# A gated layer's tiles 3 to 20: four of seven products summed in one PSUM bank, weight splits on VectorE, engine order written out

## The chip, the cores and the metric

The kernel runs on one core of one Trainium2 chip. The metric is device time in microseconds (us), here of one core. Engines in the profile: PE is TensorE's matmuls and PEld its weight loads, DVE is VectorE, ACT ScalarE, POOL GpSimd, SP the queue that issues DMAs. A difference of about 0.2% can be told from none.

## The reference

One decoder layer on x of 1024 positions by 1024 channels, all in float32: a mixer (forgetting attention, dilated attention, convolution module, output projection), and then the gated layer, which is what changes here, with 2 x 2816 = 2 x 22 x 128 columns in `w_up`:

```python
h2 = rmsnorm(x, ln2_g[l])
u = jnp.einsum('bsd,df->bsf', h2, w_up[l])
u = causal_dwconv(u, ffn_conv_w[l], ffn_conv_b[l])      # 3 taps
hidden = jax.nn.silu(u[..., :D_FF]) * u[..., D_FF:]
x = x + jnp.einsum('bsf,fd->bsd', hidden, w_down[l])
return rmsnorm(x, g_final)
```

## The kernel before

Channels lie on the 128 partitions, positions along the free dimension, in two halves of 512. Every product is made of float32 operands split in two parts, a rounded high part and the low remainder; three matmuls (high x high, high weight x low input, low weight x high input) give one product of a 128x128 weight block (`mm3`, lines 116 to 118).

The gated layer works on 22 tiles of 128 hidden channels, each with a gate half and a value half. `up` (line 891) makes tile j by Winograd's form of Strassen's product: instead of eight block products it takes seven, of weight combinations (`wsum`, line 743) with input combinations that stay in SBUF (`PROD`, line 816). Product 1 takes the input blocks `b11`, 2 `b21`, 3 `b22`, 4 to 7 `t4`, `t1`, `t2`, `t3`. Each product is 4 blocks x 3 matmuls = 12 matmuls of 512 columns into one bank of its own, so a tile is 84 matmuls. Tiles 0 to 2 have their products 1 and 2 made ahead (`early`) and issue 60.

For a tile, SP loads four raw weight blocks `a11`, `a21`, `a22`, `a12` (256 KB each) into a ring of seven slots; VectorE forms `s1`, `s2`, `a11 - a21`, `s4` from them (lines 760 to 766); for each product `wsplit` (line 821) has ScalarE cast the weights to the high part `wh` (line 827) and GpSimd subtract to get the low part `wl` (line 828). There are four buffers for `wh` and `wl`, so a split can start when the product four before it has ended. VectorE combines the seven banks into the tile's two halves `urg` (gate) and `urv` (value) with seven adds and one copy on ScalarE (lines 900 to 907). `gate` (line 930) is the convolution: on each of `urg` and `urv` one ScalarE activation (first tap and bias, line 937) and two VectorE taps (line 939), then Silu on ScalarE (line 941) and a product on VectorE (line 942). The result is kept in DRAM as blocks and combinations of two tiles, formed every second tile (lines 950 to 957), for the down projection that follows.

The order on each engine is chosen by a scheduler from program order and priority; weight loading and splitting run at high priority. Engines take their instructions in order.

```python
        for n in PORD if pre else order:
            w = wsplit(j, n, ws[n])
            M[n] = bank(f"m{n}_{j}")
            prod(M[n], n, w)
            evict()
```

Of the kernel before, what the change touches and what calls it, by code (L numbers as in the profile page):

```python
# [44 lines left out]
# pairs of hidden tiles taken together in w_down; the last NL tiles are multiplied directly  # L45
# [5 lines left out]
# columns of the packed parameter table  # L51
# [9 lines left out]
def hybrid_trunk(ctx: ExitStack, tc: tile.TileContext, xT, par, win, wvf, wo, wup, wdn,  # L61
# [87 lines left out]
    # ==== mixer =========================================================  # L149
    with ExitStack() as cb_:  # L150
# [32 lines left out]
        # x * ln1_g in two parts, and the sum of squares of x  # L183
        order = (12, 14, 13, 15)          # gv0 gg0 gv1 gg1
# [558 lines left out]
    def wsum(j, src=None, n=4):  # L743
        """the weight blocks and their combinations"""
# [58 lines left out]
    g1 = [half_pair(f"g1_{k}", "aacc"[k]) for k in range(4)]      # B12 and B22 before r2  # L803
# [17 lines left out]
    def wsplit(j, n, t, nk=4):  # L821
        with tc.high_priority():
# [26 lines left out]
    g2 = [half_pair(f"g2_{k}", "a") for k in range(4)]            # T3 and T2  # L849
# [29 lines left out]
    def slot_tile(name, shape, dt=F32):  # L879
        """a tile in any slot that is free by now"""  # L880
# [10 lines left out]
    def up(j, pre=None, order=UORD, then=lambda n: None):  # L891
        """gate and value of one tile of the hidden layer"""
# [259 lines left out]
```

## Time and profile before

| | |
|---|---|
| time, median of 3 runs (lowest, highest) | 1353.99 us (1352.52, 1354.97) |
| profiled execution: span from first to last instruction | 1351.2 us |
| what lies around the span (median less span) | 2.8 us |
| PE busy | 1251.2 us (93%), 5809 matmuls |
| PEld, DVE, ACT, POOL busy | 989.3 (73%), 1081.9 (80%), 603.4 (45%), 775.5 us (57%) |
| POOL, low parts `wl` of the up projection (line 828) | 150.3 us and 103.7 us in two groups, 84 and 66 instructions |

Busy time is an average over stages with different limits, so the stretch of tiles 3 to 20 has to be read by itself. Matmuls overlap: one lasts 0.39 us and the next begins 0.23 us after it, so the distance between starts is what a matmul costs.

### The profile page before, as it was taken

The page shows a single profiled execution, that of the slowest core. Times are in us where ns is not written, and L with a number is a line of the kernel's source. Part 1 is how long each engine was busy: PE and PEld are TensorE (multiplying, and loading weights), DVE is VectorE, ACT ScalarE, POOL GpSimd, SP SyncE. Part 2 cuts the span into 40 slices and gives each one's busy share as a digit, 9 for nine tenths or more (in the row PEclk, how much of TensorE's full clock was granted, in tenths as well). Part 3 has the DMA queues.
Part 4 walks back from the last instruction along what each step waited for, and adds up shares of the span by engine and source line. Part 5 has one row for each costly group of instructions (what it writes and reads, how often), then busy time and mean ns, then how long its engine had stood idle before and what let it go on. Part 6 is the DMA issues. An engine that isn't in the chain of part 4 may idle for free.

```text
span 1351.2 us, 17266 instructions
## 1 busy us (share of the span) xinstructions
PE 1251.2 (93%) x5809; PEld 989.3 (73%) x5809; DVE 1081.9 (80%) x1553; ACT 603.4 (45%) x1092; POOL 775.5 (57%) x607
## 2 busy tenths in 40 slices
PE   7898999999999999997798999999999979999996
PEld 5886677777777767774576877777777857787795
DVE  7899796756665676699988888888888889878876
ACT  6423456655555555434433443333423444534333
POOL 4656545554554532457555566656656577767754
PEclk9999899999999999999899999999999989999998
DMA  6002011110010203320132123231222365525213
GB/s 234 17 26 69 16 48 32 32 32 32 16 32 13 66 12 102 106 67 0 39 110 102 60 105 109 95 109 68 96 102 94 103 194 161 188 84 169 61 32 125
DMA packets 56409, 106.70 MB, mean 79 GB/s; under 512 B 5457, under 2 KB 25601, under 8 KB 56321
## 3 DMA queue, kind: packets, MB, share of 16 engines
q1 hardware_dynamic: 55744, 105.32, 23.8%
q8 instruction: 46, 0.75, 0.2%
q14 instruction: 43, 0.34, 0.1%
q10 hardware_dynamic: 576, 0.28, 0.1%
HBM read 82.75 MB, written 22.83 MB: 78 GB/s over the span
## 4 chain that ended last, share of the span: by engine, by line
PE 49%; DVE 17%; issue 16%; POOL 12%; DMA 3%; ACT 2%; POOLq 0%; DVEq 0%; SPq 0%; ACTq 0%
POOL wl L828 8%; PE m L118 4%; PE s L380 4%; PE m L116 3%; PE m L117 3%; PE pt L405 3%; PE d L118 3%; PE s L379 3%; PE d L117 3%; PE d L116 2%; DVE yc L508 2%; PE av L422 2%; PE av L421 2%; POOL VS L280 1%; DMA tr<-td 1%
## 5 line engine op out<-in xcount | busy, mean ns | idle before, releaser
L828 POOL TENSOR_TENSOR wl<-a,wh 128x512 fp32r<-128x512 f32 x84 | 150.3, 1811 | 29.0 <-ACT wh L827 29.0
L828 POOL TENSOR_TENSOR wl<-s,wh 128x512 fp32r<-128x512 f32 x66 | 103.7, 1574 | 99.8 <-ACT wh L827 99.8
L393 POOL TENSOR_SCALAR w<-w,rd 128x128 f32<-128x128 f32 (+3 forms) x96 | 77.4, 811 | 137.7 <-DVE rd L392 81.0
L117 PE MATMUL m<-t,wh 128*128 128x512 f32 x352 | 139.4, 396 | 7.5 <-DVE t L741 7.5
L116 PE MATMUL m<-t,wh 128*128 128x512 f32 x352 | 138.9, 395 | 5.0 <-ACT t L740 4.2
L118 PE MATMUL m<-t,wl 128*128 128x512 f32 x352 | 138.8, 394 | 2.5 <-POOL wl L828 2.5
L118 PE MATMUL m<-b,wl 128*128 128x512 f32 x240 | 97.5, 406 | 23.2 <-POOL wl L828 22.7
L118 PE MATMUL d<-hc,wld 128*128 128x512 f32 x252 | 102.5, 407 | 10.3 <-POOL wld L828 10.2
L410 DVE TENSOR_TENSOR pl<-pt,ph 128x512 fp32r<-128x512 f32 (+1 forms) x120 | 75.0, 635 | 38.5 <-ACT ph L409 35.3
L117 PE MATMUL d<-hc,whd 128*128 128x512 f32 x252 | 101.2, 402 | 3.6 <-DVE hc L979 3.6
L116 PE MATMUL d<-hc,whd 128*128 128x512 f32 x252 | 101.2, 402 | 2.0 <-ACT whd L827 2.0
L390 ACT ACTIVATE w<-w,mn 128x128 f32<-128x128 f32 (+3 forms) x96 | 74.4, 775 | 62.1 <-DVE mn L385 59.0
L939 DVE SCALAR_TENSOR_TENSOR cv<-urv,prm,cv 128x1023 f32<-128x1023 f32 (+1 forms) x44 | 97.7, 2221 | 0.0
L116 PE MATMUL m<-b,wh 128*128 128x512 f32 x240 | 95.5, 398 | 0.2 <-ACT wh L827 0.2
L117 PE MATMUL m<-b,wh 128*128 128x512 f32 x240 | 95.3, 397 | 0.0
L508 DVE SCALAR_TENSOR_TENSOR yc<-gv,prm,yc 128x1023 f32<-128x1023 f32 (+29 forms) x60 | 89.0, 1484 | 0.9
L827 ACT CAST wh<-s 128x512 fp32r<-128x512 f32 x66 | 39.8, 611 | 103.4 <-DVE s L762 86.9
L939 DVE SCALAR_TENSOR_TENSOR cg<-urg,prm,cg 128x1023 f32<-128x1023 f32 (+1 forms) x44 | 65.8, 1495 | 24.5 <-ACT cg L937 24.5
L117 PEld LDWEIGHTS m<-t,wh 128*128 128x128 f32 x352 | 67.0, 190 | 24.0 <-DVE t L741 10.1
L409 ACT CAST ph<-pt 128x512 fp32r<-128x512 f32 (+1 forms) x120 | 63.9, 542 | 44.4 <-PE pt L405 31.6
L116 PEld LDWEIGHTS m<-t,wh 128*128 128x128 f32 x352 | 67.0, 190 | 20.7 <-ACT t L740 4.9
L118 PEld LDWEIGHTS m<-t,wl 128*128 128x128 f32 x352 | 67.1, 191 | 17.4 <-POOL wl L828 3.8
(437 smaller groups left out, 3706.6 us busy)
## 6 DMA issues: line engine op xcount, KB each, us to landing
a<-in_wup SPq DMA_DIRECT2D x88, 256.0 KB, 2.6
tr<-td SPq DMA_DIRECT2D x27, 512.0 KB, 3.8
a_d<-in_wdn SPq DMA_DIRECT2D x48, 192.0 KB, 2.4
td<-cv SPq DMA_DIRECT2D x9, 512.0 KB, 2.6
td<-ta SPq DMA_DIRECT2D x9, 512.0 KB, 2.6
td<-tb SPq DMA_DIRECT2D x9, 512.0 KB, 2.6
x<-in_xT SPq DMA_DIRECT2D x8, 512.0 KB, 3.7
outT<-fo SPq DMA_DIRECT2D x8, 512.0 KB, 2.8
```

Of the source, the lines that this page charges most:

```text
L116: T.matmul(ps, lhsT=wh, rhs=xh[:, sl], start=first, stop=False)
L117: T.matmul(ps, lhsT=wh, rhs=xl[:, sl], start=False, stop=False)
L118: T.matmul(ps, lhsT=wl, rhs=xh[:, sl], start=False, stop=last)
L379: T.matmul(ps[:, 0:m], lhsT=Q[h][:, qsl], rhs=K[h][:, ks], start=True, stop=False)
L380: T.matmul(ps[:, 0:m], lhsT=Q[h][ro, qsl], rhs=KL[ro, ks], start=False, stop=not diag)
L390: A.activation(w[:, 0:nk], w[:, 0:nk], AF.Exp, scale=-1.0, bias=mn, accum_out=den)
L393: G.tensor_scalar(w[:, 0:nk], w[:, 0:nk], rd, 1.0, op0=ALU.mult, op1=ALU.mult)
L409: A.copy(ph[:, 0:w], pt[:, 0:w])
L410: V.tensor_sub(pl[:, 0:w], pt[:, 0:w], ph[:, 0:w].bitcast(F32))
L508: V.scalar_tensor_tensor(y[:, d:], u[:, 0:S - d], col(wc + 30 - d), y[:, d:], op0=ALU.mult, op1=ALU.add)
L828: G.tensor_sub(lo, t, hi.bitcast(F32))
L939: V.scalar_tensor_tensor(cc[:, d:], ur[:, 0:S - d], col(wc + 2 - d), cc[:, d:], op0=ALU.mult, op1=ALU.add)
```

## The change

Tiles 3 to 20 leave `up` for a new function `pipeline`, which writes out, product by product ("slot" by slot), what VectorE, ScalarE and GpSimd do. Tiles 0 to 2 and 21 stay with `up`.

- Products go in the order 1, 4, 6, 7, 5, 2, 3. Products 1, 6, 5 and 3 accumulate in one bank `mA`; only the first clears it. After each of them ScalarE copies the running sum: M1 (`u1`), M1+M6 (first half of `urv`), M1+M6+M5 (second half), M1+M6+M5+M3 (second half of `urg`). VectorE adds the other three banks: four adds in place of seven.
- The weights of a product are split three products ahead (`prep(g + FRONT)`). The low part is made by VectorE for products 6, 7, 5, 2 and 3, by GpSimd for 1 and 4.
- Weight sums, the convolution of the tile before and the stores are put into fixed slots, and the relative order on the three engines is kept by the scheduler (`manual_schedule`), which still merges other work into it. The value half is convolved before the gate half.

Core of the diff (the new `conv_first`, `conv_tap` and `store` hold the old lines of `gate`, cut apart):

```diff
-    def wsplit(j, n, t, nk=4):
+    def wsplit(j, n, t, nk=4, eng=G):
...
-            G.tensor_sub(lo, t, hi.bitcast(F32))
+            eng.tensor_sub(lo, t, hi.bitcast(F32))
...
-    def prod(ps, n, w, x=None):
+    def prod(ps, n, w, x=None, first=True, **kw):
...
-            mm3(ps, w[k], x[k], FULL, k == 0, k == len(w) - 1)
+            mm3(ps, w[k], x[k], FULL, first and k == 0, k == len(w) - 1, **kw)
...
+    SORD = (1, 4, 6, 7, 5, 2, 3)
+    FIRST, FRONT = 3, 3
+    NP = len(SORD)
+
+    def pipeline(n_last):
...
+        def prep(g):
+            j, n = FIRST + g // NP, SORD[g % NP]
+            if j < n_last:
+                hl[g] = wsplit(j, n, raw[j, SRC[n]], eng=G if (g - FRONT) % NP in (4, 5) else V)
...
+        def evict(j, k):
+
+            if k == 0:
+                M[j, "u1"] = cp.tile([P, HALF], F32, tag="rb2", name=f"u1_{j}", bufs=1)
+                A.copy(M[j, "u1"], M[j, "A"])
+            elif k == 2:
+                ur[j] = [None, ur_tile(f"urv{j}")]
+                A.copy(ur[j][1][:, HS[0]], M[j, "A"])
+            elif k == 3:
+                h0 = ur[j][1][:, HS[0]]
+                V.tensor_add(h0, M[j, 7], h0)
+                V.tensor_sub(h0, h0, M[j, 4])
+            elif k == 4:
+                h1 = ur[j][1][:, HS[1]]
+                A.copy(h1, M[j, "A"])
+                V.tensor_add(h1, M[j, 7], h1)
+            elif k == 5:
+                ur[j][0] = ur_tile(f"urg{j}")
+                V.tensor_add(ur[j][0][:, HS[0]], M[j, 2], M[j, "u1"])
+            elif k == 6:
+                A.copy(ur[j][0][:, HS[1]], M[j, "A"])
...
+        for j in range(FIRST, n_last):
+            nxt = j + 1 < n_last
+            for k, n in enumerate(SORD):
...
+                if n in (4, 7, 2):
+                    prod(M[j, n], n, hl[g])
+                else:
+                    prod(M[j, "A"], n, hl[g], first=n == 1, skip_group_check=True)
+                if k:
+                    evict(j, k - 1)
+                elif j > FIRST:
+                    evict(j - 1, 6)
...
+                prep(g + FRONT)
+                if j > FIRST and k < 4:
+                    after(j - 1, k + 1)
+                if j > FIRST and k >= 4 and tail.get(j - 1):
+                    tail[j - 1].pop(0)()
+                if k == 6:
+                    after(j, 0)
+                    if nxt:
+                        wsums(j + 1, 4)
...
-    for j in range(1, NFF - 1):
-        if j in pre:
-            pre[j]["ws"] = wsum(j)
-        up(j, pre.get(j))
+    for j in range(1, FIRST):
+        pre[j]["ws"] = wsum(j)
+        up(j, pre[j])
+    with tc.manual_schedule(engines={nc.vector.engine, nc.scalar.engine, nc.gpsimd.engine}):
+        pipeline(NFF - 1)
     ur_last = up(NFF - 1, then=release)
```

How the order moves, in rows of line, operation, out<-in and shape; a name's first number is the tile, its next the product, the last a buffer number. VectorE in tile 12 before, from the first weight sum of tile 13 to the last:

```order
L760 TENSOR_TENSOR s1_13_8194<-a21_13_8190,a22_13_8192 128x512
L939 SCALAR_TENSOR_TENSOR cv11_8014<-urv11_7884,prm_67,cv11_8014 128x1023
L763 TENSOR_TENSOR a21_13_8190<-a11_13_8188,a21_13_8190 128x512
L939 SCALAR_TENSOR_TENSOR cv11_8014<-urv11_7884,prm_67,cv11_8014 128x1022
L902 TENSOR_TENSOR sc12_8050<-m6_12_8073,sc12_8050 128x512
L942 TENSOR_TENSOR cv11_8014<-cv11_8014,cg11_8013 128x1024
L762 TENSOR_TENSOR s2_13_8196<-s1_13_8194,a11_13_8188 128x512
L952 TENSOR_TENSOR ta5_8023<-cv11_8014,cv10_7859 128x512
L953 TENSOR_TENSOR tb5_8024<-cv10_7859 128x512
L954 TENSOR_TENSOR ta5_8023<-ta5_8023,cv10_7859 128x512
L766 TENSOR_TENSOR s4_13_8201<-a12_13_8199,s2_13_8196 128x512
```

The same engine now, from product 7 of tile 12 (the fourth slot) to its last slot:

```order
L1008 TENSOR_TENSOR s1_13_8096<-a21_13_8034,a22_13_8036 128x512
L828 TENSOR_TENSOR wl12_3_8099<-s4_12_8016,wh12_3_8098 128x512
L1072 TENSOR_TENSOR cv11_8013<-cv11_8013,cg11_8012 128x1024
L1040 TENSOR_TENSOR urv12_8094<-m7_12_8081,urv12_8094 128x512
L1041 TENSOR_TENSOR urv12_8094<-urv12_8094,m4_12_8044 128x512
L1011 TENSOR_TENSOR s2_13_8118<-s1_13_8096,a11_13_8032 128x512
L961 TENSOR_TENSOR ta5_8126<-cv11_8013,cv10_7861 128x512
L962 TENSOR_TENSOR tb5_8127<-cv10_7861 128x512
L1045 TENSOR_TENSOR urv12_8094<-m7_12_8081,urv12_8094 128x512
L1013 TENSOR_TENSOR a21_13_8034<-a11_13_8032,a21_13_8034 128x512
L966 TENSOR_TENSOR ta5_8126<-ta5_8126,cv10_7861 128x512
L1048 TENSOR_TENSOR urg12_8166<-m2_12_8130,u1_12_8057 128x512
```

Before, s2 of tile 13 stood behind two taps and a product of tile 11; now the splits `wl` have come in, the adds of a tile's banks have become fewer, and the weight sums stand one to a slot. ScalarE now, in tile 12 from the cast for its product 2 on:

```order
L827 CAST wh12_2_8076<-a12_12_7987 128x512
L1037 COPY urv12_8094<-mA_12_8018 128x512
L827 CAST wh12_3_8098<-s4_12_8016 128x512
L1071 ACTIVATE cg11_8012<-cg11_8012 128x1024
L827 CAST wh13_1_8120<-a11_13_8032 128x512
L1044 COPY urv12_8094<-mA_12_8018 128x512
L827 CAST wh13_4_8148<-a22_13_8036 128x512
```

The copies of `mA` stand between casts, and one of them behind the Silu (line 1071) of the tile before; before, ScalarE copied only M1 (line 900). VectorE where tile 2 hands over to tile 3, now:

```order
L903 TENSOR_TENSOR urv2_6483<-m5_2_6544,sc2_6484 128x512
L1016 TENSOR_TENSOR s4_3_6603<-a12_3_6601,s2_3_6598 128x512
L828 TENSOR_TENSOR wl3_6_6614<-s2_3_6598,wh3_6_6613 128x512
L828 TENSOR_TENSOR wl3_7_6637<-a21_3_6592,wh3_7_6636 128x512
L904 TENSOR_TENSOR urg2_6482<-m3_2_6508,urv2_6483 128x512
L906 TENSOR_TENSOR urv2_6483<-m5_2_6544,urv2_6483 128x512
L907 TENSOR_TENSOR urv2_6483<-urv2_6483,m4_2_6564 128x512
L936 SCALAR_TENSOR_TENSOR cg2_6578<-urg2_6482,prm_67,cg2_6578 128x1023
L828 TENSOR_TENSOR wl3_5_6656<-s1_3_6596,wh3_5_6655 128x512
```

Two splits of tile 3 have moved ahead of three adds of tile 2, and a third in among its taps. Elsewhere the order is the same but for a few neighbours: at the very start ScalarE squares the first tile of x ahead of its two casts (lines 209 and 201), with both halves of its load issued first.

## Rows read from the trace of the kernel before

**Rows 1.** Busy time by stretch: us, each engine's busy us (instructions), granted clock, DMA.

```profile
core 0: us, PE busy (x) PEld busy (x) DVE busy (x) ACT busy (x) POOL busy (x), PEclk, DMA share, GB/s
...
690.74:1070.14 379.40, 353.44 (x1513) 285.77 (x1512) 324.47 (x322) 140.26 (x200) 228.43 (x137) 0.99 0.28 96
...
801.53:820.57 19.04, 19.04 (x86) 15.77 (x84) 16.63 (x17) 7.09 (x11) 9.38 (x6) 1.00 0.19 69
...
1089.34:1150.00 60.66, 51.06 (x188) 38.75 (x188) 55.91 (x68) 30.75 (x55) 44.72 (x32) 0.89 0.57 182
```

**Rows 2.** Timeline of PE (start us, us): around first matmuls of tiles 3, 8, 21.

```profile
690.51 0.39 PE L118 MATMUL m<-t,wl 128*128 128x512 f32 x1
690.74 0.39 PE L116 MATMUL m<-b,wh 128*128 128x512 f32 x1
...
801.53 0.39 PE L116 MATMUL m<-b,wh 128*128 128x512 f32 x1
801.75 0.39 PE L117 MATMUL m<-b,wh 128*128 128x512 f32 x1
...
1070.14 0.39 PE L116 MATMUL m<-b,wh 128*128 128x512 f32 x1
```

**Rows 3.** Costliest groups, whole span: xcount | busy us, mean ns | idle before.

```profile
L118 PE MATMUL m<-t,wl 128*128 128x512 f32 x352 | 138.8, 394 | 2.5 <-POOL wl L828 2.5
L118 PE MATMUL m<-b,wl 128*128 128x512 f32 x240 | 97.5, 406 | 23.2 <-POOL wl L828 22.7
```

**Rows 4.** Waits in 690.7 to 1070.1 us: total us, times, longest.

```profile
POOL wl L828 <- ACT wh L827: 106.3, 65, 5.0
ACT wh L827 <- DVE s L762: 86.9, 15, 6.2
...
PE m L118 <- POOL wl L828: 24.5, 12, 2.8
```

**Rows 5.** Durations of DVE lines: minimum/median/maximum ns, first to last start us.

```profile
L939 DVE SCALAR_TENSOR_TENSOR cv<-urv,prm,cv x44: 1269/2311/2333, 667.3 to 1136.7; 128x1023 f32<-128x1023 f32 x22, 128x1022 f32<-128x1022 f32 x22
L763 DVE TENSOR_TENSOR a<-a,a x22: 675/1774/1782, 569.1 to 1061.2; 128x512 f32<-128x512 f32 x22
L942 DVE TENSOR_TENSOR cv<-cv,cg x22: 1207/1708/2306, 676.1 to 1138.0; 128x1024 f32<-128x1024 f32 x22
L902 DVE TENSOR_TENSOR sc<-m,sc x22: 674/678/680, 659.0 to 1088.7; 128x512 f32<-128x512 f32 x22
```

**Rows 6.** Timeline of DVE, and of POOL, in 775 to 805 us.

```profile
776.27 0.68 DVE L952 TENSOR_TENSOR ta<-cv,cv 128x512 f32<-128x512 f32 x1
776.87 0.68 DVE L953 TENSOR_TENSOR tb<-cv 128x512 f32<-128x512 f32 x1
...
791.59 1.77 DVE L763 TENSOR_TENSOR a<-a,a 128x512 f32<-128x512 f32 x1
...
789.06 7.70 POOL L828 TENSOR_TENSOR wl<-a,wh 128x512 fp32r<-128x512 f32 x4 [0.35 <-ACT wh L827]
```

**Rows 7.** Groups of ACT in 690.74 to 1070.14 us, columns as in rows 3.

```profile
L827 ACT CAST wh<-a 128x512 fp32r<-128x512 f32 x72 | 42.8, 615 | 24.5 <-issue 11.9 <-POOL wl L828 6.3 <-PE m L117 6.3
...
L937 ACT ACTIVATE cg<-urg,prm 128x1024 f32<-128x1024 f32 x18 | 22.4, 1244 | 57.9 <-DVE urg L901 50.1 <-DVE urg L904 7.8
...
L941 ACT ACTIVATE cg<-cg 128x1024 f32<-128x1024 f32 x19 | 20.2, 1062 | 58.9 <-DVE cg L939 58.9
L900 ACT COPY sc<-m 128x512 f32<-128x512 f32 x18 | 10.4, 576 | 0.0
```

**Rows 8.** Group of POOL in the same stretch.

```profile
L828 POOL TENSOR_TENSOR wl<-a,wh 128x512 fp32r<-128x512 f32 x73 | 130.3, 1809 | 13.3 <-ACT wh L827 13.3
```

**Rows 9.** DMA issues: KB each, median us from issue to landing.

```profile
a<-in_wup SPq DMA_DIRECT2D x88, 256.0 KB, 2.6
```

**Rows 10.** Timeline of PE at the kernel's start.

```profile
5.04 0.76 PE L116 MATMUL gv0a<-xh,wh_w 128*128 128x512 f32 x1 [5.04 <-DVE wh_w L100]
...
9.31 0.80 PE L116 MATMUL gg0a<-xh,wh_w 128*128 128x512 f32 x1 [1.22 <-DVE wh_w L100]
```

More of the change, by code (lines that the diff above doesn't have):

```diff
@@ L111, in load_chunk, with mm3 @@
         return w
-    def mm3(ps, w, x, sl, first, last):
+    def mm3(ps, w, x, sl, first, last, **kw):
         wh, wl = w
         xh, xl = x
-        T.matmul(ps, lhsT=wh, rhs=xh[:, sl], start=first, stop=False)
-        T.matmul(ps, lhsT=wh, rhs=xl[:, sl], start=False, stop=False)
-        T.matmul(ps, lhsT=wl, rhs=xh[:, sl], start=False, stop=last)
+        T.matmul(ps, lhsT=wh, rhs=xh[:, sl], start=first, stop=False, **kw)
+        T.matmul(ps, lhsT=wh, rhs=xl[:, sl], start=False, stop=False, **kw)
+        T.matmul(ps, lhsT=wl, rhs=xh[:, sl], start=False, stop=last, **kw)
     def mm_gen(ps, ws, xs, sl):
@@ L928, in hybrid_trunk, with conv_first @@
     cvs = {}
[L930 to L937 removed]
+    def conv_first(j, ur, cc, v):
+        wc = C_FW + 3 * (NFF * v + j)
+        A.activation(cc, ur, AF.Identity, scale=col(wc + 2), bias=col(C_FB + NFF * v + j))
@@ new lines, in conv_tap, with cg_tile, cv_tile, store @@
+    def conv_tap(j, ur, cc, v, d):
+        wc = C_FW + 3 * (NFF * v + j)
+        V.scalar_tensor_tensor(cc[:, d:], ur[:, 0:S - d], col(wc + 2 - d), cc[:, d:],
+                               op0=ALU.mult, op1=ALU.add)
+    def cg_tile(j):
+        return cp.tile([P, S], F32, tag="rb", name=f"cg{j}", bufs=1)
+    def cv_tile(j):
+        cvs[j] = x_tile(f"cv{j}")
+        return cvs[j].rearrange("p i s -> p (i s)")
+    def store(j):
+        if j >= LAST:
+            return [lambda: nc.sync.dma_start(hd[j - LAST], cvs[j].rearrange("p i s -> p (i s)"))]
+        if j % 2 == 0:
+            return []
+        p, b1, b2 = j // 2, cvs.pop(j - 1), cvs.pop(j)
+        b11, b12, b21, b22 = b1[:, 0], b1[:, 1], b2[:, 0], b2[:, 1]
+        tiles = []
+        def diffs():
+            nc.sync.dma_start(td[p][:, 0, :], b11)
+            nc.sync.dma_start(td[p][:, 5:7, :], b2)
+            tiles.extend((x_tile(f"ta{p}"), x_tile(f"tb{p}")))
+            ta, tb = tiles
+            V.tensor_sub(ta[:, 1], b22, b12)
+            V.tensor_sub(tb[:, 0], b12, b11)
+        def sums():
+            ta, tb = tiles
+            V.tensor_add(ta[:, 0], ta[:, 1], b11)
+            nc.sync.dma_start(td[p][:, 1:3, :], ta)
+        def rest():
+            ta, tb = tiles
+            G.tensor_sub(tb[:, 1], ta[:, 0], b21)
+            nc.sync.dma_start(td[p][:, 3:5, :], tb)
+        return [diffs, sums, rest]
@@ new lines, in hybrid_trunk, with load, wsums, tile_of @@
+    SORD = (1, 4, 6, 7, 5, 2, 3)
+    FIRST, FRONT = 3, 3
+    NP = len(SORD)
+    def pipeline(n_last):
+        wts, hl, M, ur, raw = {}, {}, {}, {}, {}
+        tail = {}
+        def load(j, b):
+            src = {11: wup[j][:, 0:4], 12: wup[j][:, 4:8], 21: wup[NFF + j][:, 0:4], 22: wup[NFF + j][:, 4:8]}[b]
+            raw[j, b] = raw_tile(f"a{b}_{j}")
+            nc.sync.dma_start(raw[j, b], src)
+        def wsums(j, n):
+            a11, a12, a21, a22 = (raw.get((j, b)) for b in (11, 12, 21, 22))
+            if n == 1:
+                raw[j, "s1"] = raw_tile(f"s1_{j}")
+                V.tensor_add(raw[j, "s1"], a21, a22)
+            elif n == 2:
+                raw[j, "s2"] = raw_tile(f"s2_{j}")
+                V.tensor_sub(raw[j, "s2"], raw[j, "s1"], a11)
+            elif n == 3:
+                V.tensor_sub(a21, a11, a21)
+            else:
+                raw[j, "s4"] = raw_tile(f"s4_{j}")
+                V.tensor_sub(raw[j, "s4"], a12, raw[j, "s2"])
+        SRC = {1: 11, 4: 22, 6: "s2", 7: 21, 5: "s1", 2: 12, 3: "s4"}
+        def prep(g):
+            j, n = FIRST + g // NP, SORD[g % NP]
+            if j < n_last:
+                hl[g] = wsplit(j, n, raw[j, SRC[n]], eng=G if (g - FRONT) % NP in (4, 5) else V)
+        def tile_of(j):
+            if j not in ur:
+                ur[j] = [None, None]
+            return ur[j]
+        def evict(j, k):
[18 more added lines that the diff above has]
+                A.copy(ur[j][0][:, HS[1]], M[j, "A"])
+        gated = {}
+        def after(j, n):
+            urg, urv = ur[j]
+            if n == 0:
+                gated[j] = (cg_tile(j), cv_tile(j))
+            cg, cv = gated[j]
+            if n == 0:
+                conv_first(j, urv, cv, 1)
+                conv_tap(j, urv, cv, 1, 1)
+            elif n == 1:
+                conv_first(j, urg, cg, 0)
+                conv_tap(j, urv, cv, 1, 2)
+            elif n == 2:
+                conv_tap(j, urg, cg, 0, 1)
+            elif n == 3:
+                conv_tap(j, urg, cg, 0, 2)
+            elif n == 4:
+                A.activation(cg, cg, AF.Silu)
+                V.tensor_mul(cv, cv, cg)
+                tail[j] = store(j)
+        for b in (11, 21, 22):
+            load(FIRST, b)
+        for n in (1, 2, 3):
+            wsums(FIRST, n)
+        load(FIRST, 12)
+        wsums(FIRST, 4)
+        for g in range(FRONT):
+            prep(g)
+        for j in range(FIRST, n_last):
+            nxt = j + 1 < n_last
+            for k, n in enumerate(SORD):
+                g = (j - FIRST) * NP + k
+                if k == 0:
+                    M[j, "A"] = bank(f"mA_{j}")
+                elif n in (4, 7, 2):
+                    M[j, n] = bank(f"m{n}_{j}")
+                if n in (4, 7, 2):
+                    prod(M[j, n], n, hl[g])
+                else:
+                    prod(M[j, "A"], n, hl[g], first=n == 1, skip_group_check=True)
[3 more added lines that the diff above has]
+                    evict(j - 1, 6)
+                if nxt and k == 0:
+                    load(j + 1, 11)
+                    load(j + 1, 21)
+                    load(j + 1, 22)
+                if nxt and k == 3:
+                    wsums(j + 1, 1)
+                if nxt and k == 4:
+                    wsums(j + 1, 2)
+                if nxt and k == 5:
+                    load(j + 1, 12)
+                    wsums(j + 1, 3)
+                prep(g + FRONT)
[7 more added lines that the diff above has]
+                        wsums(j + 1, 4)
+        evict(n_last - 1, 6)
+        for n in range(1, 5):
+            after(n_last - 1, n)
+        for f in tail[n_last - 1]:
+            f()
```

29 lines of the change are left out of this document (6 added, 23 removed).

## The prediction

> **What bounds the kernel now.** I read the stretches first, then the matmuls at their edges, then the waits, then single durations.
>
> [Rows 1] gives busy time by stretch, and [rows 2] places the stretch that changes. Tile 3's first matmul starts at 690.74 us, tile 21's at 1070.14: with product order 1, 6, 5, 3, 2, 7, 4 a tile begins where a `b` operand (product 1) follows the `t` of product 4. The counts agree: three groups of 352 and three of 240 matmuls [rows 3] are 1776 = 3 x 60 + 19 x 84. So tiles 3 to 20 take 379.40 us, 21.08 each. Tile 8 (801.53 to 820.57) shows what TensorE needs when nothing holds it: 19.04 us for 84 matmuls, 0.2267 us each, PE busy throughout and clock 1.00 [rows 1]. Eighteen such tiles are 342.7 us, so this stretch holds 36.7 us of PE stalls, and no more can come out of it.
>
> Who makes the stalls? [Rows 4], read upwards: TensorE waits for GpSimd's low weight parts (24.5 us), GpSimd for ScalarE's high parts (106.3), ScalarE for VectorE's weight sum s2 (86.9). The root is VectorE, an in-order queue that reaches s2 late. It was busy 324.47 of 379.40 us, 18.0 per tile, and it is that busy because it runs beside GpSimd. [Rows 5] has the same instruction in two lengths: a tap 1.27 or 2.31 us, a 512-column sum of SBUF tiles 0.68 or 1.77, the gate product 1.21 or 2.31, while an add that reads a PSUM bank is always 0.68. [Rows 6] shows why: at 791.59, inside four GpSimd splits back to back, a sum takes 1.77; at 776.27, with GpSimd quiet, 0.68. The rest of the lost time is the lower clock after a stall (0.99 over the stretch), which goes with the stalls.
>
> **The change, part by part (per tile, 18 tiles).**
>
> VectorE. It gains five splits (512-column SBUF sums, 5 x 0.68 = 3.4 us) and loses three of seven PSUM adds (3 x 0.68 = 2.0). Without GpSimd in the way the new list is 4 taps x 1.27 + product 1.21 + 10.5 SBUF sums x 0.68 (4 weight sums, 5 splits, 3 store sums every second tile) + 4 PSUM adds x 0.68 = 5.1 + 1.2 + 7.1 + 2.7 = 16.1 us. The old list by the same prices is 5.1 + 1.2 + 5.5 x 0.68 + 7 x 0.68 = 14.8; 18.0 were measured, so meeting 7.5 GpSimd instructions cost 3.2 net of the small overlap between neighbours (0.60 apart, 0.68 long [rows 6]). With 2.5 left, a third: 1.1. Estimate: 17.2 us of VectorE per tile, under TensorE's 19.04. Bounds: 16.1 if they never meet; 16.1 + 2.5 x 1.81 = 20.7 if each remaining GpSimd instruction [rows 8] blocks VectorE for its whole length. I take 17.2, since the 3.2 was measured on the same mix.
>
> The row says that VectorE loses 1.1 us (1.77 less 0.68) where it meets GpSimd. The Trainium skill, page "SBUF — State Buffer", section "Who interferes with whom", speaks against giving VectorE more such sums while GpSimd still splits: an instruction with two SBUF inputs and a GpSimd instruction that reads SBUF take one port as an exclusive lock, and the later one blocks fully. The trace agrees in kind (PSUM adds stay at 0.68); read at its strictest the rule gives the 20.7 end and, as the rival below works out from rows, 1348 us; the measured mix gives 17.2 and 1318.
>
> ScalarE. Seven casts x 0.615 + four bank copies x 0.576 (one before) + 2 x 1.244 + Silu 1.062 [rows 7] = 10.2 us of 19.04. Room on average; the copies are also a new wait of TensorE. Products 1, 6, 5, 3 go to one bank with 4, 7, 2 between them, so a copy has one product (12 x 0.2267 = 2.72 us) before the bank is written again. The last matmul ends 0.16 after the next begins (0.39 long), the copy takes 0.58: 1.98 us of slack. In front of it in ScalarE's order stands at most an activation and a cast, 1.24 + 0.615 = 1.86. It fits, barely in the worst case: cost 0, and with the cover gone up to the 1.06 of a Silu per tile. Behind the waiting copy stand the next cast, needed two products later, and taps, needed by no matmul.
>
> GpSimd. 2.5 instructions x 1.81 = 4.5 us at most; its part in tiles 3 to 20 stops being late.
>
> Weight lead. A split is issued three products ahead into four buffers, so it may start when the product before the current one has ended: 3 x 2.72 = 8.2 us for a cast (0.615), a split (0.68 to 1.81) and the queue. Walking the order slot by slot with these durations, VectorE is latest after the slot with an add, a split, a tap and a sum (0.68 + 0.68 + 1.27 + 0.68 = 3.3 against 2.72); with an odd tile's store sums ahead it ends some 2 us late. A split is still made 5 us before its product. VectorE catches up in the next three slots (1.95 each). So no stall in the steady tiles, 18 x 19.04 = 342.7.
>
> SP. The same four loads per tile, 2.6 us to landing [rows 9], issued at the tile's first product and read at its fourth, 8.2 us later; a12, the last, is behind them in the queue and read three products after that. The stores move with their sums. Cost 0; cover 5 us.
>
> Tile 3. On VectorE the split for tile 3's product 7 stands ahead of three adds of tile 2. Its buffer is free only when tile 2's last product ends, so VectorE stands until then, and those adds, the four taps behind them and tile 2's product are late. The next split in that queue (product 5) comes after it, three adds and a tap: 0.68 + 4 x 0.6 + 2 x 1.24 = about 5.5 us into tile 3, needed at 4 x 2.72 = 10.9. Bounds 0, and 5.5 if this whole path stood before its product; I take 0.5, nearer to 0, since the limit is twice the path.
>
> The start and the end. ScalarE now squares the first tile of x before casting it, so the first matmul comes some 1.5 us later than 5.04; the fifth waits for its weights at 9.31 either way [rows 10], so 0, at most 1.6. After tile 21 the mixed stage at 1089.34 to 1150 keeps VectorE busy 55.91 of 60.66 us [rows 1]; tile 20's gate (4 x 1.27 + 1.21 = 6.3 us) reaches it from tile 21's time, as before. 0, within 4 us either way.
>
> **Sum.** 342.7 + 0.5 = 343.2 against 379.4: 36.2 us less. The profiled span of 1351.2 becomes 1315.0; the median of the runs, 1353.99, lies 2.8 above that span, so 1318 us. Own range 1312 to 1325.
>
> **Rivals.**
> Copies miss (1337). Where a Silu waiting for a tap stands ahead of a copy, TensorE waits about its 1.06 us once a tile: 18 x 1.06 = 19. For: 1.86 against 1.98 of slack. Against: the Silu's tap is two slots old when the copy behind it falls due.
> VectorE bound, less gain (1348). The 20.7 us end: 18 x (20.7 - 19.04) = 30 given back. For: the long rows are common now. Against: they come where four splits run back to back, and two remain.
> Slower (1380). VectorE now stands at the head of its queue for a cast before each split (5 x 0.615), for the Silu before the gate product (1.06) and for a bank copy before two adds (2 x 0.576), 5.3 us a tile. If all of it comes on top of 17.2, that is 22.5, where 21.08 decides: 18 x 1.4 = 26 lost. Against: these waits only occur while VectorE is early; if it is late, ScalarE, with 9 us a tile to spare, has long cast and copied.
> Given back at the end (1324). The 6.3 us of tile 20's gate fall wholly into the VectorE-bound stage after tile 21.
> No change (1354). A wait simply takes the place of the removed one, a weight load for example, as the order of the sums is fixed. Against: 5 us of cover.
>
> **Numbers.** Forecast 0.72, copies miss 0.12, VectorE bound 0.05, given back 0.05, slower 0.04, no change 0.02. Range 1311 to 1338: it takes in the forecast's own range, the end case and the copies case; out stay 0.11 of the cases and the fringes of the others. A measurement here tells 0.2% (2.7 us) from no change; faster by more: 0.72 + 0.12 + 0.05 + 0.05 = 0.94, within 0.02, slower 0.04.
>
> **What would show it.** Right: tiles 3 to 20 at 19.04 to 19.2 us each, granted clock 1.00 in the stretch, no wait of TensorE for `wl`, taps mostly near 1.27 us, GpSimd's busy time in the stretch down from 228 to under 85 us, ScalarE's up from 140 to about 170. Wrong: matmuls of products 6, 5 or 3 waiting for a ScalarE copy (copies rival); tiles at 20.7 with VectorE without gaps (bound); VectorE idle for casts while TensorE waits for splits (slower); tiles short but the stage after tile 21 longer than its 60.7 us by 4 or more (given back).

## The result and the profile after

The changed kernel takes **1320.84 us** (median of 4 runs, 1320.78 to 1323.55) against 1353.64 before (4 runs): ratio 0.9771, 95% interval [0.9757, 0.9785]. The profiled execution took 1320.88 us with a span of 1319.1, 32.1 under the 1351.2 of before. The forecast of 1318 lies 2.8 us under the median.

Busy time by stretch, changed kernel: tile 3, tiles 4 to 20, tile 21, the rest, and the first 60.66 us of it; columns as in [rows 1].

```profile
core 0: us, PE busy (x) PEld busy (x) DVE busy (x) ACT busy (x) POOL busy (x), PEclk, DMA share, GB/s
691.02:719.53 28.51, 21.27 (x85) 16.82 (x84) 27.38 (x33) 12.15 (x17) 6.22 (x4) 0.88 0.30 114
719.53:1043.21 323.68, 323.68 (x1429) 268.04 (x1428) 279.87 (x332) 163.12 (x238) 56.62 (x43) 1.00 0.30 105
1043.21:1062.41 19.20, 19.20 (x86) 15.92 (x85) 17.71 (x16) 11.12 (x19) 12.87 (x9) 1.00 0.47 147
1062.41:1319.10 256.69, 230.61 (x1151) 191.49 (x1149) 209.06 (x295) 104.64 (x209) 167.44 (x149) 0.95 0.39 124
...
1062.41:1123.07 60.66, 53.08 (x209) 41.83 (x208) 53.26 (x65) 31.03 (x56) 41.20 (x34) 0.89 0.51 167
```

The second line answers to the 379.40 of [rows 1]: 17 tiles in 323.68 us are 19.04 each, TensorE busy for every microsecond of it, clock 1.00. That is the floor the prediction read from tile 8. The first line is the surprise: tile 3 takes 28.51. The next view gives the edges of the stretch and both of tile 3's long waits: PE's timeline (start, us, line, idle before).

```profile
691.02 0.39 PE L116 MATMUL mA<-b,wh 128*128 128x512 f32 x1
...
695.17 0.50 PE L118 MATMUL m<-t,wl 128*128 128x512 f32 x1 [0.82 <-POOL wl L828]
...
704.16 0.80 PE L116 MATMUL mA<-t,wh 128*128 128x512 f32 x1 [6.42 <-ACT u L1034]
...
719.53 0.39 PE L116 MATMUL mA<-b,wh 128*128 128x512 f32 x1
...
1043.21 0.39 PE L116 MATMUL m<-b,wh 128*128 128x512 f32 x1
```

Where the 32.1 us come from, by these edges and [rows 2]: tile 3 starts 0.28 later (691.02 against 690.74); tiles 3 to 20 take 1043.21 - 691.02 = 352.19 against 379.40, **27.2 less**; tile 21 takes 19.20 in both; what follows it takes 256.69 against 1351.2 - 1089.34 = 261.86, **5.2 less**. So 27.2 + 5.2 - 0.28 = 32.1.

The waits in tiles 4 to 20, to be laid beside [rows 4]:

```profile
POOL wl L828 <- ACT wh L827: 260.0, 35, 14.3
...
ACT urv L1037 <- PE mA L118: 38.8, 17, 2.3
...
DVE wl L828 <- ACT wh L827: 28.5, 58, 0.9
```

The waits of before (TensorE for GpSimd, 24.5 us; ScalarE for VectorE's s2, 86.9) are gone. No line of the view has PE on its left: TensorE waits for nobody, and GpSimd, ScalarE and VectorE wait for work.

What TensorE waited for before has to be read from the timelines, though, and there it is not the weight sum s2. Four lines of the kernel before, around the start of tile 7 at 777.77 (start, us, idle before):

```profile
769.62 0.62 ACT L827 CAST wh<-a 128x512 fp32r<-128x512 f32 x1 [0.70 <-POOL wl L828]
...
778.24 1.66 POOL L955 TENSOR_TENSOR tb<-ta,cv 128x512 f32<-128x512 f32 x1 [5.30 <-DVE ta L954]
779.85 1.26 POOL L828 TENSOR_TENSOR wl<-a,wh 128x512 fp32r<-128x512 f32 x1
...
781.17 0.50 PE L118 MATMUL m<-b,wl 128*128 128x512 f32 x1 [2.78 <-POOL wl L828]
```

TensorE stands in product 1, whose weights are a raw block. Their cast was done at 770.24, but their split stands on GpSimd behind `tb` (line 955), a difference for the store of a pair of tiles, which waits 5.30 us for VectorE's store sum `ta` (line 954). Nine of the twelve waits, 22.0 of the 24.5 us, end with a split right behind `tb`: tile 3 and every odd tile from 5 to 19. VectorE's lateness is still at the root, but it reaches TensorE through GpSimd's queue. In the change the splits for products 1 and 4 of the next tile are written ahead of `tb`.

Groups of tiles 4 to 20 in the changed kernel (columns as in [rows 7]: xcount | busy, mean ns | idle before):

```profile
L936 DVE SCALAR_TENSOR_TENSOR cv<-urv,prm,cv 128x1023 f32<-128x1023 f32 (+1 forms) x36 | 46.8, 1301 | 1.1
...
L828 POOL TENSOR_TENSOR wl<-a,wh 128x512 fp32r<-128x512 f32 x33 | 43.3, 1311 | 257.5 <-ACT wh L827 257.5
...
L1013 DVE TENSOR_TENSOR a<-a,a 128x512 f32<-128x512 f32 x16 | 26.2, 1638 | 0.0
L828 DVE TENSOR_TENSOR wl<-a,wh 128x512 fp32r<-128x512 f32 x34 | 23.4, 689 | 5.9 <-ACT wh L827 5.9
...
L1037 ACT COPY urv<-mA 128x512 f32<-128x512 f32 x17 | 10.0, 587 | 38.8 <-PE mA L118 38.8
```

A tap of line 936 on the value half has come down to 1.30 us on the mean (a median of 2.31 before); one weight sum, line 1013, still meets GpSimd (1.64). It looks as if a VectorE that is no longer stretched were the reason for the gain. The experiments say otherwise.

### The profile page after: what moved, and what is told of

The parts are those of the page before. It is cut to its first block, busy times and chain, and to the rows that moved or that the text cites. A ratio compares the mean times of both kernels' runs of the same rounds, so it can differ in the third digit from the quotient of the medians.

```text
span 1319.1 us, 17062 instructions
## 1 busy us (share of the span) xinstructions
PE 1240.6 (94%) x5809; PEld 987.8 (75%) x5809; DVE 1062.8 (81%) x1589; ACT 635.9 (48%) x1146; POOL 602.6 (46%) x517
## 4 chain that ended last, share of the span: by engine, by line
PE 65%; DVE 20%; POOL 5%; issue 5%; DMA 3%; ACT 2%; SPq 0%; DVEq 0%; ACTq 0%; POOLq 0%
PE mA L116 5%; PE mA L117 5%; PE mA L118 5%; PE m L118 4%; PE m L117 4%; PE m L116 4%; PE s L380 4%; PE pt L405 3%; PE d L118 3%; PE d L117 3%; PE d L116 3%; PE s L379 3%; DVE yc L508 3%; PE av L422 2%; PE av L421 2%
## 5 line engine op out<-in xcount | busy, mean ns | idle before, releaser
L828 POOL TENSOR_TENSOR wl<-a,wh 128x512 fp32r<-128x512 f32 x48 | 69.7, 1453 | 294.6 <-ACT wh L827 282.4
L117 PE MATMUL m<-t,wh 128*128 128x512 f32 x208 | 83.0, 399 | 7.5 <-DVE t L741 7.5
L116 PE MATMUL m<-t,wh 128*128 128x512 f32 x208 | 82.2, 395 | 4.2 <-ACT t L740 4.2
L118 PE MATMUL m<-t,wl 128*128 128x512 f32 x208 | 82.5, 397 | 1.4 <-POOL wl L828 1.4
L405 PE MATMUL pt<-idf,w 128*128 128x128 f32 x432 | 70.8, 279 | 8.1 <-POOL w L393 7.7
L827 ACT CAST wh<-a 128x512 fp32r<-128x512 f32 x84 | 52.2, 621 | 41.5 <-issue 24.3
L828 POOL TENSOR_TENSOR wld<-a_d,whd 128x384 fp32r<-128x384 f32 x48 | 57.3, 1196 | 21.4 <-ACT whd L827 21.3
L422 PE MATMUL av<-pl,VS 128*128 128x256 f32 x240 | 61.1, 289 | 3.2 <-DVE pl L410 3.2
L421 PE MATMUL av<-ph,VS 128*128 128x256 f32 x240 | 63.8, 285 | 0.2
L116 PE MATMUL mA<-t,wh 128*128 128x512 f32 x144 | 56.9, 395 | 6.4 <-ACT u L1034 6.4
L405 PEld LDWEIGHTS pt<-idf,w 128*128 128x128 f32 x432 | 50.4, 142 | 15.7 <-POOL w L393 11.1
```

The costliest lines, as they stand in the source:

```text
L118: T.matmul(ps, lhsT=wl, rhs=xh[:, sl], start=False, stop=last, **kw)
L405: T.transpose(pt[:, P * b:P * b + P], ws[n][j][:, P * kt:P * kt + P], idf)
L421: T.matmul(o, lhsT=vt, rhs=phl[0][:, r], start=kt == 0, stop=False)
L422: T.matmul(o, lhsT=vt, rhs=phl[1][:, r], start=False, stop=kt == 2 * i + 1)
L828: eng.tensor_sub(lo, t, hi.bitcast(F32))
```

## The experiments

Three groups: what holds tile 3 (e1, e2, e3, e5, e12), which part of the change makes the gain (e4, e6, e7, e8, e9, e10, e11), and what is left for the stage behind tile 21 (all of them together). Runs of one kernel spread by as much as 0.7% (e6: 1317.22 to 1326.04), so the tiles are read from the traces, by the starts of their first matmuls as above.

### Which part makes the gain

**e4: all splits on GpSimd, lead kept.**

```diff
-                hl[g] = wsplit(j, n, raw[j, SRC[n]], eng=G if (g - FRONT) % NP in (4, 5) else V)
+                hl[g] = wsplit(j, n, raw[j, SRC[n]], eng=G)
```

> The changed kernel with the weight splits of tiles 3 to 20 back on GpSimd, all seven of a tile, still written three products ahead. Theory of contention (GpSimd's splits stretch VectorE's sums, taps and products by about 1.1 us each time they meet): VectorE gives up 5 x 0.69 = 3.4 us a tile and gains 5 to 6 meetings, 5.5 to 6.6 us, so it goes from 17.6 to about 20 us a tile and bounds the tiles at 19.5 to 20.5: 17 tiles cost 8 to 25 us more, the kernel 1330 to 1345. Rival (GpSimd was late only because the scheduler put its splits late; written early they are in time whoever makes them): tiles stay at 19.04 and the kernel at 1319 to 1322.

Measured: 1321.95 us, ratio 0.9779 [0.9759, 0.9799]: no different from the change. Tiles 4 to 20 by the view of stretches, and two groups in them:

```profile
721.47:1045.15 323.68, 323.68 (x1430) 268.02 (x1428) 280.73 (x248) 163.02 (x238) 194.93 (x127) 1.00 0.30 105
```

```profile
L828 POOL TENSOR_TENSOR wl<-a,wh 128x512 fp32r<-128x512 f32 x67 | 108.8, 1624 | 71.8 <-ACT wh L827 71.3 <-DVE s L760 0.6
...
L936 DVE SCALAR_TENSOR_TENSOR cg<-urg,prm,cg 128x1023 f32<-128x1023 f32 (+1 forms) x34 | 72.2, 2125 | 3.3 <-ACT cg L932 2.8
```

The contention is back: the gate half's taps of line 936 are at 2.13 us on the mean (1.28 in the change), and VectorE is as busy (280.73) with 248 instructions as it was with 332 (279.87), so what the 5 x 17 splits took away the meetings gave back. And not one tile is longer than 19.04. The theory of contention falls: in this code who makes the splits does not matter once they are written three products ahead.

**e6: the same program, order left to the scheduler.**

```diff
-    with tc.manual_schedule(engines={nc.vector.engine, nc.scalar.engine, nc.gpsimd.engine}):
+    if True:
         pipeline(NFF - 1)
```

> The changed kernel without the order written out: the same instructions of tiles 3 to 20 (four products in one bank, splits mostly on VectorE, three products ahead in the code), put in order by the scheduler. Theory of order (since e4 left every tile at 19.04 with the splits on GpSimd, it is the place of the sums and splits in the order that takes the wait for weights away): the stalls come back, 20 to 21.5 us a tile, the kernel 1335 to 1360. Rival (fewer adds and the splits' early place in the code do it): 19.04 to 19.3 us a tile, the kernel 1319 to 1326.

Measured: 1321.31 us, 0.9775 [0.9739, 0.9811], tiles 4 to 20 again 19.04 each:

```profile
715.36:1039.04 323.68, 323.68 (x1429) 268.11 (x1428) 268.80 (x332) 164.10 (x239) 58.99 (x43) 1.00 0.31 105
```

The rival holds: the written order is not needed either.

**e7: the four copies of the summed bank on VectorE** (`A.copy` becomes `V.tensor_copy` in the four places of `evict`).

> The changed kernel with the four copies of the summed bank on VectorE, so that VectorE reads PSUM eight times a tile as often as before the change. VectorE gains 4 x 0.6 = 2.4 us a tile on 16.46 busy, 18.9 of 19.04. If the bank sums matter because VectorE would else be the bound, tiles take 19.3 to 20.5 us and the kernel 1326 to 1346. Rival (slack of 2.6 us takes them in): tiles at 19.04, tile 3 2 to 3 us longer since VectorE is behind there, the kernel 1320 to 1325.

Measured: 1320.78 us, 0.9771 [0.9741, 0.9801], 19.04 a tile:

```profile
717.61:1041.29 323.68, 323.68 (x1430) 268.11 (x1428) 307.50 (x399) 130.26 (x170) 56.58 (x43) 1.00 0.30 106
```

VectorE at 307.50 of 323.68 us, 18.1 a tile, more than the 18.0 of before, and TensorE does not wait. So VectorE's load was not the bound, and sparing it three adds of a bank is not what the bank sums are worth here. Tile 3 took 27.76 us, not longer as the rival had it.

**e8: the kernel before with five of seven splits on VectorE.**

```diff
-            w = wsplit(j, n, ws[n])
+            w = wsplit(j, n, ws[n], eng=V if 3 <= j < NFF - 1 and n not in order[:2] else G)
```

> The kernel before with one part of the change alone: five of the seven weight splits of a tile, from tile 3 to 20, on VectorE. Theory of order: the scheduler still puts the sums and splits late on a VectorE that now has 3.4 us more, so the wait for weights stays; tiles 20.5 to 22.5 us, the kernel 1345 to 1380. Rival (GpSimd's slow splits were the cause): tiles at 19.1 to 20, the kernel 1320 to 1335.

Measured: 1335.33 us, 0.9877 [0.9849, 0.9905]: at the edge of the rival's range. Tiles 3 to 20 take 1051.09 - 690.88 = 360.21 us, 20.0 each; even tiles from 6 on stand at 19.04, odd ones lose 1.6 to 1.8 at their last product. The waits of PE in that stretch:

```profile
PE m L118 <- DVE wl L828: 12.7, 11, 1.5
PE m L118 <- POOL wl L828: 0.7, 1, 0.7
```

Without a lead, moving the splits gives half of the gain. Why is not settled by this run: with the edit the scheduler has also put product 1's split ahead of `tb` on GpSimd (tile 7: 765.03 against 772.01), so that the sparing of GpSimd and the new order there come together. The wait for weights is still there, now for VectorE, where a split stands behind taps and a gate product.

**e9: the kernel before with the product order of the change** (1, 4, 6, 7, 5, 2, 3 for tiles 3 to 20).

> The kernel before with one part of the change alone: tiles 3 to 20 take their seven products in the order 1, 4, 6, 7, 5, 2, 3 in place of 1, 6, 5, 3, 2, 7, 4, so that the second product needs no weight sum. Its 3 us stalls stand at the second product of every other tile, for the split of the second weight sum. Theory (the sums come too late by 3 us, one product is 2.72 us): most of them go, 19.1 to 20 us a tile, the kernel 1320 to 1337. Rival (the sums are late by the scheduler's order and the wait only moves to the product that then needs a sum): 20.5 to 21.5 us, the kernel 1345 to 1360.

Measured: 1354.67 us, 1.0024 [1.0007, 1.0041]. Tiles 3 to 20 take 1072.59 - 693.98 = 378.61 us, 21.0 each. The rival holds in size, but the place is neither its own nor the theory's: in the traces the long waits of the odd tiles from 5 on stood at the first product before and stand at the second, product 4, now, and neither needs a weight sum. As before, the split stands on GpSimd behind `tb` (nine of the fourteen waits, 18.7 of 20.4 us):

```profile
PE m L118 <- POOL wl L828: 20.4, 14, 2.7
POOL tb L955 <- DVE ta L954: 33.3, 8, 4.2
```

**e10: no lead, written order, splits on GpSimd.**

```diff
-    FIRST, FRONT = 3, 3
+    FIRST, FRONT = 3, 0
...
                 g = (j - FIRST) * NP + k
+                prep(g + FRONT)
...
-                prep(g + FRONT)
```

(and `eng=G`, as in e4)

> The changed kernel without the lead of its splits: each weight's split is written just ahead of its own product instead of three products ahead, all on GpSimd as before the change; the order stays written out. Theory (the lead of three products is what takes the wait for weights away): a split of 1.3 to 2.3 us behind its cast of 0.6 on a ScalarE that first waits for bank copies comes late once or more in a tile, 20 to 24 us a tile, the kernel 1338 to 1410. Rival (the sums' early slots are enough): 19.04 to 19.3, the kernel 1319 to 1326.

Measured: 1375.54 us, 1.0161 [1.0129, 1.0192]. Tiles 4 to 20 take 374.05 us, 22.0 each, and every one of them waits twice (the busy time by stretch, and the waits of PE):

```profile
718.59:1092.64 374.05, 338.54 (x1429) 263.42 (x1428) 280.23 (x247) 160.68 (x241) 209.07 (x129) 1.00 0.26 92
```

```profile
PE mA L118 <- POOL wl L828: 24.2, 25, 1.2
PE m L118 <- POOL wl L828: 10.8, 9, 1.2
```

Against e4 only the lead is gone: 50.4 us over 17 tiles (374.05 - 323.68), with the same instructions, engines and order of sums.

**e11: no lead, order by the scheduler, splits on GpSimd** (the edits of e10 and e6).

> As e10_no_lead, and the order is left to the scheduler, which gives weight splits priority, as before the change; what stays of the change is the four products in one bank, the product order and the sums' place in the code. If the lead in the code decides, the stalls of before come back, 20 to 22 us a tile, the kernel 1337 to 1372. If bank sums, product order or the sums' place do: 19.04 to 19.4, the kernel 1319 to 1328.

Measured: 1355.83 us, 1.0025 [1.0008, 1.0042]. Tiles 4 to 20 take 1075.65 - 717.75 = 357.90 us, 21.05 each, the 21.08 of before. But the wait is another one:

```profile
PE mA L116 <- ACT urv L1037: 20.3, 11, 2.9
```

ScalarE's timeline in tile 17 shows why (start, us, idle before): the copy of the bank stands behind a Silu that waited 6.06 us for VectorE's tap.

```profile
1000.73 1.06 ACT L1071 ACTIVATE cg<-cg 128x1024 f32<-128x1024 f32 x1 [6.06 <-DVE cg L936]
...
1002.72 0.58 ACT L1037 COPY urv<-mA 128x512 f32<-128x512 f32 x1
```

Together: with the lead, four kernels (the change, e4, e6, e7) stand at the floor, with the engine of the splits, the engine of the copies and who orders changed one at a time; without it, four kernels with GpSimd's splits (before, e9, e10, e11) stand at 21.0 to 22.0, the one with VectorE's (e8) at 20.0. In the new code the lead of three products makes the gain in the tiles; e4 against e10 shows it, with the lead alone removed. Two things were not tried. One is the lead with seven separate banks, so whether the bank sums are needed at all (seven of eight banks would be taken by a tile) stays open. The other is the old code with nothing but `tb` moved behind product 1's split: 22.0 of its 24.5 us of waits stand there, so this small edit is an untested rival for the old kernel.

### What holds tile 3

ScalarE and VectorE in tile 3 of the changed kernel, from the timeline:

```profile
702.39 1.24 ACT L932 ACTIVATE cg<-urg,prm 128x1024 f32<-128x1024 f32 x1 [8.69 <-DVE urg L904]
703.54 0.56 ACT L1034 COPY u<-mA 128x512 f32<-128x512 f32 x1
...
701.02 0.68 DVE L828 TENSOR_TENSOR wl<-a,wh 128x512 fp32r<-128x512 f32 x1
701.62 0.68 DVE L904 TENSOR_TENSOR urg<-m,urv 128x512 f32<-128x512 f32 x1
```

Product 6 goes into the bank of product 1 and waits for its copy (line 1034). The copy stands behind the first activation of tile 2's gate, which waited 8.69 us for VectorE's third-last add of tile 2, begun at 701.62, 10.6 us after tile 3's first matmul. VectorE did not stand; it was busy 27.38 of 28.51 us, with the taps of tile 1 until 694. Tiles 1 and 2 take 14.55 and 13.60 us of TensorE (five products each), and VectorE has a whole gate to do for each.

**e1: tile 2's gate written into tile 3's slots behind the copy, and the copy into a buffer that is free.** Core of it:

```diff
+                if j == FIRST:
+                    M[j, "u1"] = left[FIRST - 1]
+                else:
+                    M[j, "u1"] = cp.tile([P, HALF], F32, tag="rb2", name=f"u1_{j}", bufs=1)
...
                 prep(g + FRONT)
+                if j == FIRST:
+                    gate_by(k)
```

> The changed kernel, with tile 2's gate written into slots 1 to 5 of tile 3 behind tile 3's first bank copy, and that copy put into the half of tile 2's scratch tile that is read last before 694.6 us, so that it waits neither for ScalarE's first activation of tile 2's gate nor for a buffer. Theory A (ScalarE's written order holds the bank, and VectorE's backlog stands right behind it): product 6 of tile 3 then waits for VectorE's split of its weights, which ended at 701.1 us against a start of 704.16 now, so tile 3 takes 24 to 26 us in place of 28.5 and the kernel about 1317.5 us. Theory B (VectorE's backlog alone sets it): tile 3 stays within 1 us of 28.5 and the kernel at 1321. Theory C (ScalarE's order alone sets it): tile 3 takes 19 to 20.5 us and the kernel 1312.

Measured: 1318.67 us, 0.9753 [0.9729, 0.9778]; tile 3 takes 719.33 - 693.97 = 25.36 us, 3.15 less. Waits of PE:

```profile
PE mA L118 <- DVE wl L828: 3.0, 1, 3.0
PE m L118 <- POOL wl L828: 0.8, 1, 0.8
```

Theory A holds in place and size: the copy is out of the way, and VectorE's split for the same product stands behind it.

**e2: e1, and tile 3's splits on GpSimd** (`eng=G if j == FIRST or ...`).

> As e1_junction, and besides all seven weight splits of tile 3 go to GpSimd, which stands idle for 15 of the 28.5 us of tile 3. Theory A (order first, VectorE's backlog second): both causes are gone, tile 3 takes 20 to 22 us and the kernel about 1313.5 us. Theory C (order alone): no more than e1_junction, 1312 for both. Theory B (backlog alone): 5 splits of 0.69 us leave VectorE, tile 3 takes about 25 us and the kernel 1317.5.

Measured: 1318.95 us, 0.9752 [0.9724, 0.9779]; tile 3 takes 718.49 - 692.31 = 26.18 us. Theory A fails here:

```profile
PE mA L116 <- ACT urv L1041: 2.6, 1, 2.6
PE m L118 <- POOL wl L828: 1.9, 2, 1.3
```

Now product 5 waits for the bank's second copy, whose target buffer VectorE's second tap of tile 2 has not yet released.

**e3: tile 3's splits on GpSimd and nothing else.**

> The changed kernel with all seven weight splits of tile 3 on GpSimd and nothing else moved. Theory A (ScalarE's order holds the bank until VectorE's add of tile 2 at 701.62): only the two splits ahead of that add leave VectorE, 1.2 us, so tile 3 takes 27 to 27.6 us and the kernel about 1319.7. Theory B (backlog alone): all five count, 3.4 us, the kernel 1317.4. Theory C says what A says.

Measured: 1320.95 us, 0.9772 [0.9745, 0.98]; tile 3 takes 28.99 us, not less than 28.51. Theory B (backlog alone) falls: with the copy where it is, less work for VectorE buys nothing. But the 27 to 27.6 us of theories A and C were missed too. VectorE's add comes earlier here (698.23, 9.9 us into the tile), yet ScalarE's second activation of tile 2 now also stands ahead of the copy, and TensorE waits 7.2 us for it.

**e5: e1, and two differences, a sum and a gate product moved from VectorE to GpSimd** (`store` of the first pair, the product of tile 2).

> As e1_junction, with work taken off VectorE at the place where it is behind: the two differences and the sum of the first pair of hidden tiles (3 x 0.68 us ahead of tile 3's first split on VectorE) and the product with the gate of tile 2 go to GpSimd, idle there. Theory A' (what is left of tile 3's loss is VectorE's backlog, passed on as whichever wait comes first): product 6 waits 1 us in place of 3.0, and tile 3 takes 22.5 to 24 us against 25.4 of e1_junction, the kernel about 1316.5. Rival (another chain, such as the buffers of the hidden tile, sets it): tile 3 stays at 25 to 26.

Measured: 1317.21 us, 0.9744 [0.9711, 0.9777]; tile 3 takes 714.54 - 688.46 = 26.08 us. As the rival says: the wait for the split halves to 1.6, and the wait for the buffer takes its place.

```profile
PE mA L116 <- ACT urv L1042: 2.0, 1, 2.0
PE mA L118 <- DVE wl L828: 1.6, 1, 1.6
```

**e12: e1, product 6's split on GpSimd, and product 2 ahead of product 5 in tile 3.** In this edit the copy for the second half of tile 3's value stands behind product 3, so that half holds products 1, 6, 5 and 3 in place of 1, 6 and 5: the kernel does not compute the layer, and product 3 has one wait less. Its time is read with that.

> e1_junction with two more edits in tile 3 alone, aimed at the waits that e1, e2 and e5 showed in turn: the split of product 6's weights on GpSimd (in e1 the product waited 3.0 us for VectorE's), and product 2 ahead of product 5, so that the summed bank's second copy, which waits for VectorE's taps of tile 2 to release a buffer, has one more product (2.72 us) to be done (in e2 and e5 that wait was 2.2 to 2.8 us). Theory (VectorE's backlog of some 10 us reaches TensorE by these three ways, and each can be covered): tile 3 takes 20.5 to 23 us, the kernel 1313 to 1316. Rival (a backlog that VectorE cannot work off in tile 3 finds another way): 25 to 26.5 us, the kernel 1317 to 1319.

Measured: 1319.47 us, 0.9752 [0.9738, 0.9766]. Tile 3 takes 713.74 - 691.24 = 22.50 us as the theory says, but tile 4 takes 737.73 - 713.74 = 23.99, in place of 19.04:

```profile
PE mA L116 <- ACT u L1044: 3.0, 1, 3.0
PE m L118 <- DVE wl L828: 1.4, 1, 1.4
```

The rival holds in substance: the wait left tile 3 and came back in tile 4. Tiles 3 and 4 together: 47.55 us in the change, 44.40 in e1, 45.22 in e2, 45.12 in e5, 46.49 in e12. Of the orders tried, e1's gives the most back, some 3 us; in the others the wait only changed its place. By its median e5 is the fastest kernel of all, but its interval overlaps those of e1 and the change.

### Behind tile 21

From the end of tile 21 to the end of the span: before 261.86 us, e8 261.84 and e9 265.49 (both the old code); the change 256.69, e4 257.25, e6 257.16, e10 258.36, e11 257.95. So by one trace each the 5 us come with the new code for tiles 3 to 20, and neither with the engine of the splits, nor the written order, nor the lead. Some 2 of the 5 us lie right at the joint. Before, TensorE stood there for a cast of ScalarE, which came behind a cast that waited for stored hidden blocks to be read back (`tr<-td`):

```profile
1090.22 0.62 ACT L978 CAST hc<-tr 128x512 fp32r<-128x512 f32 x1 [4.33 <-DMA tr<-td]
1090.75 0.51 ACT L827 CAST whd<-a_d 128x384 fp32r<-128x384 f32 x1
...
1091.31 0.50 PE L116 MATMUL d<-hc,whd 128*128 128x512 f32 x1 [1.97 <-ACT whd L827]
```

In the change that cast runs at 1059.08, 3.3 us before tile 21 ends, and TensorE goes on without a wait. Why the blocks are read earlier, and where the other 3 us come from, was not settled; e9, the longest, has no such wait at the joint.

## Why the prediction was right, and where it was not

- **The steady tiles: right.** Forecast 19.04 a tile and no stall; 17 of 18 tiles measure that. The step that carried it, the weight lead of 8.2 us against a split made within 3, is the one that e10 confirms by taking it away (in e11, also without lead, it is a bank copy that comes late).
- **The root of the stalls: half right.** The prediction named VectorE, busy because it runs beside GpSimd, and took the path over the weight sum s2 and ScalarE's casts. VectorE was late, but 22.0 of the 24.5 us came by another path: its store sum held `tb` on GpSimd, and the next split stood behind that. The change removes this path as well, so the forecast held in spite of this step. And e4 has the long taps back and e7 has a busier VectorE than before, both without one stall in tiles 4 to 20: lateness, not load, made the stalls.
- **The rest of the lost time: only in part the lower clock.** Of the 36.7 us, 379.40 - 353.44 = 26.0 are idle time; the clock of 0.99 makes about 4 more (1% of the stretch, an estimate). What is left goes with the waits themselves: in e10, at clock 1.00, the tiles lose 50.4 us with 35.0 us of waits.
- **VectorE at 17.2 us a tile: too high, and without effect.** 279.87 / 17 = 16.46, near the lower bound of 16.1. The strict reading of the Trainium skill ("SBUF — State Buffer", "Who interferes with whom"), which gave the 20.7 end, did not come about. The kind it describes is in the rows: sums of two SBUF tiles at 1.64 us or taps at 2.13 where GpSimd splits, adds that read a bank at 0.69.
- **ScalarE's copies at cost 0: right for tiles 4 to 20.** No wait of PE for them. The rival "copies miss" is nonetheless a real mechanism: in e11, without lead or written order, it costs 20.3 us in 11 waits, and in tile 17, the one shown, at the very place it named: a copy behind a Silu that waits for a tap.
- **Tile 3 at 0.5 us, bounds 0 to 5.5: the step that failed.** Measured 28.51 - 19.04 = 9.47. The prediction let VectorE stand at the split for product 7 until tile 2's last product ended, and followed VectorE's own queue only. That split ran at 701.02 without a wait; VectorE was 10 us behind instead. And the path to TensorE led through ScalarE, whose order at the joint has an activation of tile 2 ahead of the first bank copy. Of the 9.47, waits are 0.82 + 6.42; most of the rest is the lower clock behind the second (the next 12 matmuls took 4.47 us in place of 2.72).
- **The end at 0 within 4: outside its bound.** It gained 5.2, so that the miss of 9.0 in tile 3 and this one partly cancel: 36.2 us forecast, 32.1 measured. That 1318 lies within 2.8 us of the median is in part luck. The start was +0.28 (0 to 1.6).
- **GpSimd, SP: right.** GpSimd 56.62 / 17 = 3.3 us a tile (at most 4.5 forecast); the longest wait for a weight load in tiles 4 to 20 is 0.5 us.

## What to carry to other kernels

When a busy engine makes another wait, ask first how far ahead its work is issued: three products of lead took all stalls of tiles 4 to 20 away here, in e7 with VectorE as busy as before, while moving the splits to VectorE without a lead (e8) took half. Then look at what stands just ahead of the awaited instruction in the queue of its engine: before, it was a store difference that had nothing to do with the weights. Where a new schedule takes over from an old one, walk every engine's queue across the joint, the one with room included, since one activation at the head of ScalarE's order cost 3.15 us of tile 3 (e1). And a backlog that is not worked off was not hidden here by mending the wait that shows: each mend of tile 3 brought up the next wait.

## What the runs showed of the hardware

- In this mix VectorE's time beside GpSimd is traded about one for one: 85 splits moved from VectorE to GpSimd (e4) left VectorE's busy time where it was, 280.73 against 279.87 us. In sum the meetings with GpSimd cost as much as doing the splits.
- After TensorE had stood for 6.42 us in tile 3, its matmuls ran at the lower clock for a while: the granted clock was 0.50 (1.2 GHz) from 704.16 to 707.31, the first matmul 0.80 us long in place of 0.39. With two waits of at most 1.2 us in every tile (e10) it stayed at 1.00.
- A wait costs more than its idle time even at clock 1.00: 34 waits of 35.0 us in all lengthened 17 tiles by 50.4 us (e10), 0.45 more for each.
- Profiled executions begin tile 0 between 626.96 us (e6) and 634.09 (e1), though nothing that these edits name lies ahead of it. That spread of 7 us is larger than the differences between the kernels with the lead, so the stretches, not the medians, tell them apart.
